# Attention scores on one core: which engine waits for the last stores at the end of the kernel

## The chip, the cores and the metric

The kernel runs on one core of a Trainium2 chip. The metric is the device time of one execution in microseconds. A core has five engines that each run their own list of instructions: TensorE (PE, with its weight loads listed apart as PEld), VectorE (DVE), ScalarE (ACT), GpSimd (POOL) and SyncE (SP). They meet only through semaphores: counters that an instruction or a DMA raises, and for which another instruction can wait.

## The reference

For each of 8 batches and 8 heads, the scores of 512 queries against 512 keys of 64 numbers, scaled by 1/8, all in float32:

```python
q = randn(8, 8, 512, 64); k = randn(8, 8, 512, 64)          # float32
scale = 1.0 / np.sqrt(q.shape[-1])
return np.einsum('bhqd,bhkd->bhqk', q, k) * scale           # (8, 8, 512, 512) float32
```

The inputs are 16.78 MB together, the output is 67.11 MB.

## The kernel before

The kernel uses no scheduler for its main part: each engine's list is written out by hand, one engine after the other in the source, with named semaphores between them (the function opens at the top of the file; all lines below are lines of the kernel before).

The batches are taken in 4 units of two batches. For each unit, SP loads 2 MB of k and 2 MB of q (L78, eight loads in all; the last two from L92). POOL casts each load to bf16 and regroups it (L122). PE turns the cast data by transposes against an identity (L130), DVE and ACT move the turned pieces out of PSUM into the operands kT and qz (L184). From these, PE makes the scores: 16 groups, each of 8 pairs of 128x512 products (L145). ACT takes the even pairs out of PSUM and DVE the odd ones, with the scale applied on the way (L209 and L212), into one of three store buffers named big. When both have finished a group, SP issues one store of 4 MB for it (L95 waits, L96 issues). So there are 16 stores, and store g raises the semaphore `store_sems[g % 3]` by 16 when it has landed.

The order on the engines' queues around the change is this:

- SP's list is: the loads, then 16 times a wait for ACT and DVE and a store, then the loop of L98 and L99, which waits for the final count of each of the three store semaphores (96, 80 and 80). In the program built from it these three waits are two instructions: one for the second store semaphore, one for the third and the first together. Nothing stands behind them on SP.
- PE's list is: a wait for the identity (L149), the first transposes, then the 16 groups of products with the transposes of later chunks between them. The last thing in it is the last product of group 15. PE already waits for earlier stores inside the groups (in `scores`, before the second product of a group), since a store buffer can be filled again only when its store has landed.
- ACT, DVE and POOL end with their last evacuation or cast, and none of them waits for the last stores.

What comes after an engine's last instruction of the kernel is not in the source: it belongs to the runtime, and shows in the trace only by the semaphores that it changes.

Of the kernel before, what the change touches and what calls it, by code (L numbers as in the profile page):

```python
# [5 lines left out]
def kernel(  # L6
# [5 lines left out]
    nc = tc.nc  # L12
# [27 lines left out]
    store_sems = [nc.alloc_semaphore(f"store{n}") for n in range(3)]  # L40
    ALL = CHUNKS * UNITS
# [24 lines left out]
    pe = nc.tensor  # L66
# [26 lines left out]
    for g in range(ALL):  # L93
# [1 line left out]
        nc.sync.wait_ge(sem["dve"], 4 * g + 4)  # L95
        nc.sync.dma_start(out=out_r[g], in_=store_buffer(g).rearrange("p x i k -> p x (i k)")  # L96
                          ).then_inc(store_sems[g % 3], 16)
    for n in range(3):  # L98
        nc.sync.wait_ge(store_sems[n], 16 * len(range(n, ALL, 3)))  # L99


    nc.gpsimd.memset(identity, 0.0).then_inc(sem["ident"], 1)  # L102
    nc.gpsimd.wait_ge(sem["ident"], 1)
# [24 lines left out]
    def turn(c, dst):  # L128
        for w in range(W):
            ins = pe.transpose(out=dst[:, w], identity=identity, in_=xw[:, c % SLOTS * W + w])  # L130
        ins.then_inc(sem["turn"], 1)

    def scores(g, p):
        x, i = p // 4, p % 4 * 2
        n = g % (2 * TILES) * 2 + x
        pair = PAIRS * g + p
        if pair >= 3:
            pe.wait_ge(sem["act" if p % 2 else "dve"], (pair - 3) // 2 + 1)
        for w in range(2):
            if p == 0 and w == 1:  # L140
                if g < 3:
                    pe.wait_ge(sem["ready"], (2, 6, 8)[g])
                else:
                    pe.wait_ge(store_sems[g % 3], g // 3 * 16)
            ins = pe.matmul(out=pss[pair % 3][:, w, :], lhsT=qz[:, n, i + w], rhs=keys[:, n],  # L145
                            start=True, stop=True)
        ins.then_inc(sem["pe_dve" if p % 2 else "pe_act"], 1)
# [7 lines left out]
    for g in range(ALL):  # L155
        c = g + CHUNKS
        for p in range(3):
            scores(g, p)
        if c < ALL:
            pe.wait_ge(sem["ready"], c // 2 + 1)  # L160
            turn(c, tp)
        for p in range(3, PAIRS):
            scores(g, p)
        if c < ALL:
            pe.wait_ge(sem["moved"], 4 * c + 4)

# [76 lines left out]
```

## Time and profile before

| what | before |
|---|---|
| median of 4 runs | 201.37 us (201.27 to 201.44) |
| the profiled execution's own time | 201.34 us |
| its span, from the first to the last instruction of the kernel | 200.0 us |
| mean granted clock of TensorE | 0.827 |
| busy: PE / DVE / ACT / POOL | 48% / 53% / 42% / 20% of the span |
| DMA moved | 83.95 MB, mean 420 GB/s |

The profile is one execution. Its page gives the busy time of each engine, the span cut in 40 slices with the busy share of engines and DMA in tenths, the DMA queues, the chain of work that ended last, and the costliest groups of instructions. Waiting instructions of a sequencer don't count as busy; they are listed when one asks for a source line or for the waits of SP's queue. Beside instructions, the trace records every change of a semaphore with its time, also those of the runtime before and after the kernel's own instructions.

### The profile page before, as it was taken

The page shows a single profiled execution, that of the slowest core. Times are in us where ns is not written, and L with a number is a line of the kernel's source. Part 1 is how long each engine was busy: PE and PEld are TensorE (multiplying, and loading weights), DVE is VectorE, ACT ScalarE, POOL GpSimd, SP SyncE. Part 2 cuts the span into 40 slices and gives each one's busy share as a digit, 9 for nine tenths or more (in the row PEclk, how much of TensorE's full clock was granted, in tenths as well). Part 3 has the DMA queues.
Part 4 walks back from the last instruction along what each step waited for, and adds up shares of the span by engine and source line. Part 5 has one row for each costly group of instructions (what it writes and reads, how often), then busy time and mean ns, then how long its engine had stood idle before and what let it go on. Part 6 is the DMA issues. An engine that isn't in the chain of part 4 may idle for free.

```text
span 200.0 us, 1081 instructions
## 1 busy us (share of the span) xinstructions
PE 96.4 (48%) x377; PEld 44.9 (22%) x384; DVE 106.0 (53%) x98; ACT 84.8 (42%) x97; POOL 39.5 (20%) x22
## 2 busy tenths in 40 slices
PE   0027550376785637576457636872737383810000
PEld 0026310142432214143124303330202020200000
DVE  0666790076797928476927682867363544440000
ACT  0205760264694726465626653664444443520000
POOL 0399999996000000000000000000000000000000
PEclk9999996588799978789958995799696969685555
DMA  6999999999999999999999999999999999999996
GB/s 193 426 436 429 439 419 432 429 410 426 432 442 426 419 434 437 432 419 429 436 436 426 419 442 442 423 419 439 439 429 419 432 432 429 429 419 439 423 432 269
DMA packets 5509, 83.95 MB, mean 420 GB/s; under 512 B 384, under 2 KB 384, under 8 KB 384
## 3 DMA queue, kind: packets, MB, share of 16 engines
q1 hardware_dynamic: 5504, 83.89, 98.6%
q8 instruction: 3, 0.05, 0.1%
q14 instruction: 2, 0.02, 0.0%
HBM read 16.78 MB, written 67.11 MB: 419 GB/s over the span
## 4 chain that ended last, share of the span: by engine, by line
DMA 54%; DVE 12%; POOL 12%; PE 10%; issue 1%; SPq 0%
DMA out_dram<-big 42%; POOL xb L122 12%; DVE big L212 10%; DMA big<-in_q_dram 7%; PE ps L145 7%; DMA big<-in_k_dram 4%; PE tp L130 2%; DVE qz L184 2%; DVE kT L184 1%; SPq L95 0%; SPq L87 0%; SPq L82 0%
## 5 line engine op out<-in xcount | busy, mean ns | idle before, releaser
L145 PE MATMUL ps<-kT,qz 128*128 128x512 bf16 x249 | 78.2, 445 | 64.8 <-DMA out_dram<-big 32.0
L212 DVE TENSOR_SCALAR big<-ps 128x1024 f32<-128x1024 f32 x64 | 76.9, 1222 | 53.2 <-PE ps L145 51.2
L209 ACT ACTIVATE big<-ps 128x1024 f32<-128x1024 f32 x64 | 65.0, 1024 | 72.2 <-PE ps L145 68.8
L145 PEld LDWEIGHTS ps<-kT,qz 128*128 128x128 bf16 x256 | 24.6, 108 | 111.4 <-DMA out_dram<-big 35.4
L122 POOL CAST xb<-big 128x2048 bf16<-128x2048 f32 x16 | 38.8, 2465 | 3.5 <-DMA big<-in_k_dram 3.0
L130 PE MATMUL tp<-identity,xb 128*128 128x128 f32 x104 | 18.8, 341 | 13.7 <-POOL xb L122 13.7
L130 PEld LDWEIGHTS tp<-identity,xb 128*128 128x128 f32 x104 | 17.1, 183 | 17.7 <-issue 16.5
L184 DVE COPY kT<-tp 64x512 f32<-64x512 f32 x14 | 9.7, 694 | 5.9 <-PE tp L130 5.4
L184 ACT COPY kT<-tp 64x512 f32<-64x512 f32 x14 | 8.1, 577 | 11.0 <-PE tp L130 10.7
L184 DVE COPY qz<-tp 64x512 f32<-64x512 f32 x12 | 8.3, 695 | 4.4 <-PE tp L130 4.0
L189 DVE MEMSET qz<- 128x4096 uint32 x2 | 6.9, 3472 | 6.8 <-PEq L87 6.0
L184 ACT COPY qz<-tp 64x512 f32<-64x512 f32 x12 | 7.4, 619 | 1.9 <-PE tp L130 1.8
L130 PE MATMUL ps<-identity,xb 128*128 128x128 f32 x24 | 3.9, 324 | 1.2 <-POOL xb L122 1.2
L130 PEld LDWEIGHTS ps<-identity,xb 128*128 128x128 f32 x24 | 3.5, 170 | 1.6 <-POOL xb L122 1.6
L184 ACT ACT_TABLE_LOAD x1 | 1.3, 1283 | 5.0 <-PEq L87 5.0
L184 DVE COPY qz<-ps 64x512 f32<-64x512 f32 x4 | 2.8, 695 | 0.9 <-PE ps L130 0.8
L184 ACT COPY qz<-ps 64x512 f32<-64x512 f32 x4 | 2.5, 624 | 1.1 <-PE ps L130 1.1
L184 DVE COPY kT<-ps 64x512 f32<-64x512 f32 x2 | 1.4, 694 | 0.3 <-PE ps L130 0.3
L184 ACT COPY kT<-ps 64x512 f32<-64x512 f32 x2 | 1.2, 578 | 0.6 <-PE ps L130 0.5
L102 POOL MEMSET identity<- 128x128 f32 x1 | 0.2, 204 | 4.6 <-POOLq L87 4.6
L104 POOL TENSOR_SCALAR_AFFINE_SELECT identity<-identity 128x128 f32<-128x128 f32 x1 | 0.3, 292 | 0.2 <-POOL identity L102 0.2
L229 POOL MEMSET const-float32-0.0<- 128x1 f32 x1 | 0.1, 98 | 0.2 <-issue 0.2
(3 smaller groups left out, 0.3 us busy)
## 6 DMA issues: line engine op xcount, KB each, us to landing
out_dram<-big SPq DMA_DIRECT2D x16, 4096.0 KB, 21.8
big<-in_k_dram SPq DMA_DIRECT2D x4, 2048.0 KB, 15.6
big<-in_q_dram SPq DMA_DIRECT2D x4, 2048.0 KB, 17.9
```

The source lines that it names most:

```text
L102: nc.gpsimd.memset(identity, 0.0).then_inc(sem["ident"], 1)
L104: nc.gpsimd.affine_select(out=identity, in_=identity, compare_op=mybir.AluOpType.not_equal, fill=1.0, base=0, pattern=[[-1, P]], channel_m ...
L122: cast = nc.gpsimd.tensor_copy(out=dst, in_=src)
L130: ins = pe.transpose(out=dst[:, w], identity=identity, in_=xw[:, c % SLOTS * W + w])
L145: ins = pe.matmul(out=pss[pair % 3][:, w, :], lhsT=qz[:, n, i + w], rhs=keys[:, n], start=True, stop=True)
L184: copy(out=dst, in_=src[:, h]).then_inc(sem["moved"], 1)
L189: engine.memset(qz[:, v * N:(v + 1) * N], 0.0).then_inc(sem["zeroed"], 1)
L209: lambda o, ps: nc.scalar.mul(out=o, in_=ps, mul=scale),
L212: lambda o, ps: nc.vector.tensor_scalar(out=o, in0=ps, scalar1=scale, scalar2=None, op0=mult),
L229: nc = _bacc.Bacc("TRN2", target_bir_lowering=False, num_devices=1)
```

## The change

The loop with the three final waits is taken from the end of SP's list and put at the end of PE's list. SP's list then ends with the issue of the last store. PE's list ends with two waiting instructions, the same pair as SP had: one for the second store semaphore, one for the third and the first. Nothing else is changed; the lists of ACT, DVE and POOL and all instructions ahead of the waits are the same.

```diff
@@ -95,9 +95,6 @@
         nc.sync.wait_ge(sem["dve"], 4 * g + 4)
         nc.sync.dma_start(out=out_r[g], in_=store_buffer(g).rearrange("p x i k -> p x (i k)")
                           ).then_inc(store_sems[g % 3], 16)
-    for n in range(3):
-        nc.sync.wait_ge(store_sems[n], 16 * len(range(n, ALL, 3)))
-
 
     nc.gpsimd.memset(identity, 0.0).then_inc(sem["ident"], 1)
     nc.gpsimd.wait_ge(sem["ident"], 1)
@@ -165,6 +162,10 @@
             pe.wait_ge(sem["moved"], 4 * c + 4)
 
 
+    for n in range(3):
+        pe.wait_ge(store_sems[n], 16 * len(range(n, ALL, 3)))
+
+
 
     def move(copy, c, s, tile_):
```

## The prediction

> **What bounds the kernel now.** I read the page's slices first, then the waits of SP's queue, then the waiting line itself, then the trace's record of semaphore changes behind the last instruction. The page, with the rows of PE, of its granted clock and of the DMA engines, and the main queue:
>
> ```profile
> span 200.0 us, 1081 instructions
> ...
> PE   0027550376785637576457636872737383810000
> ...
> PEclk9999996588799978789958995799696969685555
> DMA  6999999999999999999999999999999999999996
> ...
> q1 hardware_dynamic: 5504, 83.89, 98.6%
> q8 instruction: 3, 0.05, 0.1%
> ```
>
> The DMA row is full from the second slice to the last but one: the 84 MB set the time, and no engine does. PE's last four slices (5 us each) are empty. The end by stretches (us; busy time and count of PE, PEld, DVE, ACT, POOL; PE's clock; DMA share; GB/s):
>
> ```profile
> 178.00:198.00 20.00, 0.00 (x0) 0.00 (x0) 0.00 (x0) 0.00 (x0) 0.00 (x0) 0.51 1.00 427
> 198.00:200.00 2.00, 0.00 (x0) 0.00 (x0) 0.00 (x0) 0.00 (x0) 0.00 (x0) 0.50 0.12 49
> ```
>
> For the last 22 us nothing runs but the stores. The waits of SP's own queue (us in total, times, longest), and then the instructions of the line that the change takes away (shortest/median/longest in ns, start of the first and of the last in us):
>
> ```profile
> SPq L95 <- DVE big L212: 142.2, 16, 16.7
> ...
> SPq L99 <- DMA out_dram<-big: 22.1, 2, 19.4
> ```
>
> ```profile
> L99 SPq EVENT_SEMAPHORE  x2: 17/4852/9686, 180.6 to 190.3; - x2
> ```
>
> The first of the two waits passes at 180.6, the second is listed from 190.3 for 9.686 us, to 200.03, which is the end of the span. It has nothing to do but see the last store land.
>
> So the change can't touch the first 200 us. What it can move is the stretch behind the last landing: the profiled execution took 201.34 us, 1.34 more than its span. The record of semaphore changes shows what lies there. The last of the 16 steps of the first store semaphore comes at 200.006. Semaphore 2, which no line of the kernel uses, changes at these times (us from the span's start, listed by me from the trace):
>
> ```
> before the kernel      -0.371 -0.337 -0.299 -0.255 -0.231 -0.120 -0.081 -0.047  0.000
> first after it        176.174 176.742 176.780 177.629 200.149 200.193 200.231 200.265 200.312
> second after it       201.105 201.139 201.178 201.222 201.245 201.343 201.381 201.415 201.462
> ```
>
> Nine changes each time: a roll call of five engines, up in four steps and back in four. The first one after the kernel tells their order, since each engine answers when its list is empty and the one ahead has answered. 176.174 is 0.165 us after the step of PE's last product (176.009). 176.742 is 0.109 after ACT's last step (176.633). 176.780 follows 0.038 later and is POOL, idle for long. 177.629 is 0.145 after DVE's last (177.484). 200.149 is 0.143 after the last landing and is SP. So **the order is PE, ACT, POOL, DVE, SP, and back**. Between the two roll calls about 50 semaphores an engine are cleared; the last of the block 3 to 53, which starts latest and goes on longest, is cleared at 200.881, and PE, released last at 200.312, fits it.
>
> **The change part by part.**
>
> *Two waits leave SP.* Nothing is queued behind them, so SP is free for its answer at about 177.95 (last issue at 177.55, lasting 0.37, by the timeline). It gains nothing by that: its answer is the fifth, and waits for the four others. Cost 0; what covers it is the last store, 22 us.
>
> *Two waits come to PE.* Nothing of the kernel stands behind them, and PE's last product is done at 176.0. The first wait, passed at 180.6, lies beside 19.4 us of stores still under way: 0. The second passes when SP's did, at 200.006 plus PE's own lag. No instruction, DMA or queue moves otherwise, so all stores start and land as before: 0.
>
> *The answers behind the last landing.* Before, four of five had answered under the last stores; from the landing at 200.006 to the end of the first roll call at 200.312 it took 0.306 us (0.143 until SP answers, 0.163 for the four steps back). After, PE is late, it is the first in the row, and nobody behind it can answer. Three prices are needed.
>
> The lag of PE from landing to its answer does not stand in the trace as such. The waits that open the kernel show PE against the others (L87, same columns as above):
>
> ```profile
> L87 SPq EVENT_SEMAPHORE  x2: 17/17/17, 4.6 to 5.0; - x2
> L87 ACTq EVENT_SEMAPHORE  x2: 17/17/17, 4.6 to 5.0; - x2
> L87 DVEq EVENT_SEMAPHORE  x2: 21/21/21, 4.6 to 5.0; - x2
> L87 PEldq EVENT_SEMAPHORE  x2: 51/51/51, 4.6 to 5.0; - x2
> ```
>
> All four wait for one semaphore, raised at 4.537; the next instruction starts at 4.645 on SP and at 4.716 on PE, 0.071 later. After the roll call, SP starts to clear 0.135 after its release and PE 0.221: 0.086 later. From PE's last clear to its answer in the second roll call it is 0.224, after its last product 0.165. Bounds: 0.165 and 0.143 + 0.086 = 0.229. I take 0.143 + 0.071, about 0.215, since a wait that ends is the nearest row.
>
> The whole roll call from PE's answer to PE's release: 0.357 in the second (201.105 to 201.462), 0.371 before the kernel. A lower bound comes from adding the quickest step of each kind, 0.034 + 0.038 + 0.044 + 0.023 up and the 0.163 back of the first one: 0.302. I take 0.357, which is whole and without a wait in it.
>
> *Sum.* After: 0.215 + 0.357 = 0.572 from landing to release; before: 0.306. Difference **+0.27 us**, between 0.165 + 0.302 - 0.306 = +0.16 and 0.229 + 0.371 - 0.306 = +0.29. PE is released last and clears last in both kernels, so all behind it moves by the same. On the profiled execution that is 201.34 + 0.27 = 201.61; it lies 0.03 below the median, so 201.37 + 0.27 = **201.64 us**, 0.13% more. I count changes of up to 0.2% (0.40 us) as no change, about what a measurement of this kernel can tell.
>
> [...]
>
> **The rivals.**
>
> *A, the measured time ends before the roll call.* Then only PE's longer wait counts: its instruction lasts 51 ns against 17, and starts 11 ns later: +0.05, 201.42 us. Against it: the measured 201.34 reaches 1.31 beyond the last wait, nearly as far as the last answer at 201.46. For it: nothing in the profile says where the clock of the metric stops.
>
> *B, PE's sequencer slows down with the granted clock (the slower side).* The clock is 0.50 from 178 on, and it was 9 or more tenths in the rows at 4 to 5 us from which I took the lag. If everything of PE's answer took twice as long, its lag would be 0.43 and the total +0.27 + 0.215 = +0.49, 201.86 us; it decides from a lag of about 0.35. Against it: PE's first clear (0.221 after release) and its lag of 0.224 both fall at the 0.50 clock and are no longer than that.
>
> *C, PE has to fetch instructions behind the wait.* The queue named instruction moved three packets of 16 KB, in 0.88 to 0.99 us each, at 52.0, 97.4 and 150.6 us, when PE had 201, 450 and 687 recorded instructions behind it. If the next fetch fell behind the wait and nothing were fetched ahead, it would add up to 0.99: 202.6 us. Against it: the distance is 237 to 249 instructions, PE ends at 780, the clears add some 50, and the next fetch is due only near 924; two more instructions don't reach it.
>
> *D, I have the row of engines the wrong way round.* If PE answered last and SP first, the change would hide up the way what it now exposes, at most -0.16, 201.2 us. Against it: an SP that was first would have held back all of the answers at 176 and 177 us.
>
> **How the numbers follow.** Forecast: 0.68, of which 0.06 ends over 0.40 with the spread of the runs (0.17 between lowest and highest before). A: 0.08, within 0.2%. B: 0.13 and C: 0.05, slower. D: 0.06, half of it within 0.2% and half faster, should more be hidden than I can see. Same: 0.62 + 0.08 + 0.03 = 0.73; slower: 0.06 + 0.13 + 0.05 = 0.24; faster: 0.03. The range goes from A less the spread below the median before (201.42 - 0.09 = 201.33) to B with some of the spread (201.86 + 0.09 = 201.95); it leaves out C and D, and a little of B and of the forecast.
>
> **What would show it.** The span should grow by about 0.05 only, to 200.1, with the last instruction PE's wait of about 9.7 us from 190.3 in place of SP's, and the DMA row as full as before. In the semaphore record, the first roll call should lie wholly behind the last landing: first answer 0.17 to 0.23 after it, the whole 0.36 long, in even steps; clears and second roll call as long as before. An answer at 176 or 177 us would break the order that I read; a first answer over 0.35 after the landing is B, and an instruction packet behind 180 us is C. If stores land at another pace, the forecast is wrong in a place that I have put at nothing.

## The result and the profile after

| what | before | after |
|---|---|---|
| median | 201.41 us (201.27 to 202.32, 51 runs) | 201.71 us (201.53 to 202.32, 31 runs) |
| ratio to before | | 1.0016 (95% interval 1.0011 to 1.0021) |
| the profiled execution's own time | 201.34 us | 201.62 us |
| its span | 200.0 us | 200.0 us |
| time minus span, mean over the runs | 1.31 us (31 runs) | 1.58 us (32 runs) |

The change makes the kernel 0.30 us slower by the medians, 0.15%. That is within the 0.2% that was counted as no change, though the interval reaches to 0.21%. The kernel before was measured further beside the change, which is why its median here is 201.41 and not 201.37. The last row is the one to look at. It takes each run's own time and subtracts that run's own span, so a run whose stores happened to take longer doesn't disturb it. For the kernel before it is taken from the 31 runs measured beside the first four experiments, since the spans of the 51 are not on record. Behind the span, the change costs 1.58 - 1.31 = 0.27 us.

The page after the change, with the rows that answer to those of before:

```profile
span 200.0 us, 1081 instructions
...
PE   0027672386664768554864466662747475840000
...
PEclk9999998569999797996699697999585858585555
DMA  6999999999999999999999999999999999999996
...
q1 hardware_dynamic: 5504, 83.89, 98.7%
q8 instruction: 3, 0.05, 0.1%
```

The DMA row is as full as before, and the same three packets of instructions are there. PE's row differs in places, but its last four slices are as empty as before. The line that now waits, on PE in place of SP (shortest/median/longest in ns, first and last start in us):

```profile
L166 PEldq EVENT_SEMAPHORE  x2: 51/4868/9686, 180.6 to 190.3; - x2
```

It is the same pair of instructions as SP had, with the same 9.686 us of waiting; only the short one shows the engine, 51 ns against SP's 17. The waits of SP's queue no longer have a line for the final wait:

```profile
SPq L95 <- DVE big L213: 143.1, 16, 14.2
SPq L78 <- POOL xb L119: 23.1, 2, 18.5
SPq L230 <- PEq L230: 0.7, 1, 0.7
SPq L87 <- PEq L87: 0.5, 2, 0.3
```

So the page and the span of the profiled execution say that nothing happened. What did happen lies behind them, in the record of semaphore 2, the runtime's roll call. Here it is counted from the last step of the first store semaphore (200.006 before, 199.990 after), in us:

```
             PE        ACT       POOL      DVE       SP     | DVE    POOL   ACT    PE (release)
before      -23.832   -23.264   -23.226   -22.377    0.143  | 0.187  0.225  0.259  0.306
after         0.224     0.258     0.296     0.341    0.364  | 0.461  0.501  0.535  0.581
```

Before, four answers were given more than 22 us ahead of the last landing, and only the fifth and the way back were left. After, the whole row stands behind the landing, because the engine that asks first is the one that waits. PE is released 0.581 us after the landing and not 0.306: 0.275 us later. From there both go on alike: to PE's last clear (of the semaphores 3 to 53) it is 0.569 us before and 0.563 after. One stretch behind that differs in this profile: from its last clear to its answer in the second roll call PE takes 0.254 us and not 0.224. In the second profile of the change it is 0.224 again.

### The profile page after: what moved, and what is told of

The parts are those of the page before. It is cut to its first block, busy times and chain, and to the rows that moved or that the text cites. A ratio compares the mean times of both kernels' runs of the same rounds, so it can differ in the third digit from the quotient of the medians.

```text
span 200.0 us, 1081 instructions
## 1 busy us (share of the span) xinstructions
PE 103.0 (51%) x377; PEld 48.4 (24%) x384; DVE 106.1 (53%) x98; ACT 84.9 (42%) x97; POOL 39.5 (20%) x22
## 4 chain that ended last, share of the span: by engine, by line
DMA 54%; POOL 12%; DVE 11%; PE 11%; issue 1%; SPq 0%
DMA out_dram<-big 43%; POOL xb L119 12%; PE ps L142 9%; DVE big L213 8%; DMA big<-in_q_dram 7%; DMA big<-in_k_dram 4%; DVE qz L185 2%; PE tp L127 2%; DVE kT L185 1%; SPq L95 0%; SPq L87 0%; SPq L82 0%
## 5 line engine op out<-in xcount | busy, mean ns | idle before, releaser
L142 PE MATMUL ps<-kT,qz 128*128 128x512 bf16 x249 | 82.7, 470 | 59.2 <-DMA out_dram<-big 31.0
L142 PEld LDWEIGHTS ps<-kT,qz 128*128 128x128 bf16 x256 | 26.2, 112 | 108.8 <-DMA out_dram<-big 34.2
L127 PE MATMUL tp<-identity,xb 128*128 128x128 f32 x104 | 19.3, 348 | 13.8 <-POOL xb L119 13.8
L127 PE MATMUL ps<-identity,xb 128*128 128x128 f32 x24 | 5.6, 421 | 1.1 <-POOL xb L119 1.1
L127 PEld LDWEIGHTS ps<-identity,xb 128*128 128x128 f32 x24 | 5.0, 226 | 1.5 <-POOL xb L119 1.5
```

## The experiments

All are given with the same measures from their profile: the lag from the landing to the waiting engine's answer, the time from the landing to PE's release, and from there to PE's last clear. "Behind the span" is the mean of time minus span over all runs of a kernel. The kernel before, measured beside them, had 1.31 to 1.33 in each set.

| run | who is late | lag | landing to release | release to last clear | behind the span | median (before beside it) |
|---|---|---|---|---|---|---|
| before | SP | 0.143 | 0.306 | 0.569 | 1.31 | 201.41 |
| after | PE | 0.224 | 0.581 | 0.563 | 1.58 | 201.71 (201.41) |
| e1_act | ACT | 0.141 | 0.465 | 0.567 | 1.48 | 201.61 (201.41) |
| e2_dve | DVE | 0.182 | 0.423 | 0.565 | 1.42 | 201.49 (201.41) |
| e3_pool | POOL | 0.556 | 0.840 | 0.566 | 1.84 | 201.91 (201.41) |
| e4_pe_and_sp | PE and SP | 0.254 | 0.611 | 0.563 | 1.59 | 201.66 (201.41) |
| e5_pe_early | SP | 0.143 | 0.306 | 0.564 | 1.31 | 201.49 (201.37) |
| e6_warm_pe_waits | PE | 0.224 | 0.581 | 0.563 | 1.60 | 202.26 (201.37) |
| e7_warm_sp_waits | SP | 0.143 | 0.306 | 0.568 | 1.35 | 201.92 (201.37) |
| e8_change_again | PE | 0.224 | 0.581 | 0.563 | 1.58 | 201.80 (201.37) |
| e9_warm_40 | SP | 0.143 | 0.306 | 0.569 | 1.30 | 201.60 (201.38) |
| e10_fetch_only | SP | 0.142 | 0.306 | 0.562 | 1.34 | 202.07 (201.38) |
| e11_pool_awake | POOL | see below | 1.314 | 0.572 | 1.83 | 202.45 (201.38) |
| e12_waits_80 | SP | 0.142 | 0.306 | 0.563 | 1.31 | 201.62 (201.51) |

The theory was that an engine's place in the roll call, and its own lag, set the price. The first rival was that SP has to be the last, so that any other engine costs the same.

**The wait on each of the other engines.** The three lines leave SP and stand at the end of another engine's list (shown for ACT; with nc.vector for DVE and nc.gpsimd for POOL):

```diff
-    for n in range(3):
-        nc.sync.wait_ge(store_sems[n], 16 * len(range(n, ALL, 3)))
+    for n in range(3):
+        nc.scalar.wait_ge(store_sems[n], 16 * len(range(n, ALL, 3)))
```

On ACT:

> ScalarE, not TensorE, waits for the last stores. Theory (place in the roll call): ScalarE is second of five. Its lag from landing to answer is about SP's, 0.143 us, plus 0.005 (in the waits that open the kernel its next instruction starts at 4.650, SP's at 4.645); the roll call from its answer on lasts 0.357 - 0.034 = 0.323. Landing to PE's release: 0.47 us, against 0.306 before and 0.581 after the change; total +0.16 against before, about 201.57. Rival (SP must be last, whichever other engine waits costs the same): 0.58 and +0.28, about 201.69.

On DVE:

> VectorE waits for the last stores. Theory: fourth of five; lag 0.143 + 0.031 (its next instruction at 4.676 against SP's 4.645) = 0.174, and the roll call from its answer on 0.357 - 0.034 - 0.038 - 0.044 = 0.241. Landing to PE's release 0.415 us; total +0.11, about 201.52. Rival (SP must be last): 0.58 and +0.28, about 201.69.

On POOL:

> GpSimd waits for the last stores. Theory: third of five; lag taken as ScalarE's, 0.148, and the roll call from its answer on 0.357 - 0.034 - 0.038 = 0.285. Landing to PE's release 0.43 us; total +0.13, about 201.54. Rival (SP must be last): 0.58 and +0.28, about 201.69.

The waiting line of the three kernels, ACT, DVE and POOL:

```profile
L214 ACTq EVENT_SEMAPHORE  x2: 17/4852/9686, 180.7 to 190.4; - x2
```

```profile
L214 DVEq EVENT_SEMAPHORE  x2: 21/4850/9678, 180.6 to 190.3; - x2
```

```profile
L123 POOLq EVENT_SEMAPHORE  x2: 17/4856/9695, 180.8 to 190.5; - x2
```

These are the same two waits again, and nothing in the lines tells the three kernels apart beyond some ns. The record of semaphore 2 does, again from the last landing:

```
             PE        ACT       POOL      DVE       SP     | DVE    POOL   ACT    PE (release)
e1_act      -23.744     0.141     0.180     0.224    0.247  | 0.345  0.384  0.418  0.465
e2_dve      -22.813   -22.245   -22.207     0.182    0.205  | 0.303  0.342  0.376  0.423
e3_pool     -23.818   -23.327     0.556     0.600    0.623  | 0.720  0.760  0.794  0.840
```

The number of answers that are already in before the landing is one, three and two: the engine that waits is second, fourth and third. That confirms the order, each engine by its own kernel. For ACT and DVE the times are those expected, 0.465 for 0.47 and 0.423 for 0.415; the rival's 0.58 falls.

POOL is a miss. From its answer on, the rest of the row took 0.284 us, as worked out (0.285). Its lag, though, was 0.556 and not 0.148, so that POOL costs 0.53 behind the span, more than PE, although PE stands ahead of it. The place in the row is thus only one part of the price. The other is what an engine needs between its last instruction and its answer, and for POOL I had taken ACT's without a row of POOL's own.

**Both PE and SP wait.** SP keeps its waits, PE gets the same at the end of its list:

```diff
+    for n in range(3):
+        pe.wait_ge(store_sems[n], 16 * len(range(n, ALL, 3)))
```

> Both TensorE and SyncE wait for the last stores. Theory: TensorE alone decides, SP's early answer was worth nothing: as after the change, landing to PE's release 0.58 us, about 201.71. Rival (it is SP's early end that costs, by what SP or the runtime then does under the last stores): as before, 0.31 us, about 201.41.

Landing to release was 0.611 us, and 1.59 behind the span. PE alone decides, and SP's early end is worth nothing and costs nothing. PE's lag was 0.254 here, 0.03 more than in the three other profiles in which PE is late. PE's wait ends 0.034 us after the landing here as in the profile after the change, so the 0.03 lies between the end of the wait and the answer. The same two values, 0.224 and 0.254, stand ahead of PE's answer in the second roll call of the profiles before and after (in e6 and e10 it is 0.315 and 0.314 there); what decides between them was not found.

**PE waits, but not for the last.** As before, with two waits more on PE (one instruction in the program):

```diff
+    for n in (1, 2):
+        pe.wait_ge(store_sems[n], 16 * len(range(n, ALL, 3)))
```

> As before the change, SP waits for all three store semaphores, and TensorE waits as well, but only for the two that are complete by 190.3 us, not for the last store. Theory: waits on TensorE that pass 10 us before the last landing cost nothing: landing to PE's release 0.306 us, first four answers of the roll call under the last store, about 201.41. Rival (TensorE's added instructions cost by themselves, by more to fetch or to decode): 0.4 to 0.58 us and up to +0.28.

The first four answers lie 9.3 to 9.4 us ahead of the landing, and then it goes as before: 0.306, and 1.31 behind the span. The median was 201.49 against 201.37; with 1.31 behind the span, that difference is in the span itself (200.22 on average against 200.09), of which more below. The price is not in the waits on PE, but in their passing last.

**PE kept at work ahead of the end.** The changed kernel and the kernel before, both with 100 transposes more:

```diff
+    for w in range(100):
+        pe.transpose(out=tp[:, w % W], identity=identity, in_=identity)
```

> The changed kernel with 100 extra transposes of the identity into the free tile tp on TensorE ahead of its final waits (their result is used by nobody), so that it works until some 10 to 20 us after its last product. Theory: TensorE's lag is its sequencer's and does not depend on what the array did: lag 0.22, landing to release 0.58, about 201.71. Rival (the lag and TensorE's clears come from the long rest at the 0.50 clock): lag down to 0.15 or less and the stretch from release to last clear (0.563 after the change) down by 0.1 or more, 201.5 or less. Also, TensorE now passes the instruction at which the next packet of 16 KB is due; if it is fetched, it should be fetched during the transposes and cost nothing.

> The kernel before with the same 100 extra transposes on TensorE after its last product (their result is used by nobody); SP waits. Theory: TensorE still answers first, some 10 to 20 us later but under the last store; landing to release 0.306, release to last clear 0.569, about 201.41. Rival (TensorE's clears are slow from the long rest): release to last clear down by 0.1 or more, 201.3 or less.

From the second kernel's page:

```profile
PE   0027550475795639755767636762738283999300
```

The line of its transposes (shortest/median/longest in ns, first and last start in us):

```profile
L167 PE MATMUL tp<-identity x100: 272/273/273, 176.0 to 186.8; 128*128 128x128 f32 x100
```

PE works for 11 us longer, up to 187.0 in this kernel. PE's lag is the same in the first of the two kernels, 0.224, and the stretch of its clears within 5 ns in both, 0.563 and 0.568. So a rest of some 13 us instead of some 24 makes no difference to them; a PE that has hardly rested was not tried. What I wanted to see as well, PE at full clock when the store lands, was not reached: the records have it at 0.50 again from 190.7 (e6) and 191.9 (e7) on. What remains against rival B is that the lag of 0.224, at 0.50, is close to the 0.215 that I had worked out from rows at nine tenths. But both kernels have a longer span, 200.66 and 200.60 us on average against 200.09, which no theory had expected. The page has the packets of instructions as follows:

```profile
q8 instruction: 4, 0.07, 0.1%
```

The fourth packet, of 16 KB, moved at 187.6 us for 0.89 us. It came when PE's 987 or 988 recorded instructions were behind it, not at 924. It looked like the cause: a store has landed with the last of its 16 steps, and these are not even. In the kernel before, the sixteen steps of the last store come at 198.3 to 198.8 for twelve of them, and at 199.25, 199.53, 199.66 and 200.01 for four.

**The change once more.**

> The change itself once more, on the chip of these runs and with a second profile. Theory: landing to TensorE's answer 0.22, landing to release 0.58 us, release to last clear 0.56, +0.28 to +0.30 against before. Rival (the 0.28 was one profile's chance): the stretches differ by more than 0.05 from the first profile's.

All stretches repeat, 0.224, 0.581, 0.563, and 1.58 behind the span. The total is a miss: the medians differ by 0.43 us (201.80 against 201.37, 0.21%) and not by 0.28 to 0.30. Of that, 0.27 lies behind the span and 0.15 in it, of which more below.

**What made the span longer.** Three kernels, each from the kernel before, with SP waiting: 40 transposes, then 210 and 80 instructions that only look at semaphores (shown for 210; two waits make one instruction in the program):

```diff
+    for w in range(40):
+        pe.transpose(out=tp[:, w % W], identity=identity, in_=identity)
```

```diff
+    for w in range(210):
+        pe.wait_ge(sem["ident"], 2)
+        pe.wait_ge(sem["zeroed"], 2)
```

> The kernel before with 40 extra transposes of the identity into tp after TensorE's last product (result used by nobody) instead of the 100 that made the span 0.5 us longer; SP waits. With 40, TensorE ends 80 instructions later, at about 860, short of the fourth 16 KB packet of instructions. Theory (that packet holds up some of the 16 DMA engines, and the last store lands when the last of them is done): no fourth packet, the last landing as before, near 200.0, span 200.1, 201.4 us. Rival (the transposes themselves slow the stores): the span grows by 40% of 0.5 us, 200.3, 201.6 us.

> The kernel before with 210 instructions at the end of TensorE's list that only wait for semaphores whose counts were reached long ago (ident and zeroed); SP waits. No array work is added. Theory (the fourth packet of instructions holds up DMA engines): a fourth packet of 16 KB behind 176 us, the last landing at 200.5, span 200.6, 201.9 us. Rival (transposes slow the stores): span 200.1, 201.4 us.

> The kernel before with 80 instructions at the end of TensorE's list that only wait for counts reached long ago; SP waits. No array work, and TensorE ends short of the fourth packet of instructions. Theory (the span grows with the number of instructions that run beside the last stores, whatever they do: 80 transposed instructions gave +0.2 us, 200 to 210 gave +0.5 to +0.6): span 200.3, 201.6 us. Rival (two causes, the array work of the 40 transposes there and the packet in the run with 210 waits): span 200.1, 201.4 us.

The 40 transposes gave a mean span of 200.31 +- 0.02 against 200.09 +- 0.02 (standard errors of the means), with three packets: my theory of the packet fell. The 210 waits gave 200.72 with four packets, and with no array work at all: the rival fell too. The 80 waits, with three packets and no array work, gave 200.33 +- 0.03 against 200.19 +- 0.03 beside them. So some 80 instructions of either kind make the span 0.1 to 0.2 us longer, and 200 or 210 make it 0.5 to 0.6 us longer.

The traces also show when the stores fall behind. These are the times from one landing to the next for the last four stores, in us, beside the time at which PE's added instructions are done:

```
                  added work done    13th to 14th   14th to 15th   15th to 16th store
before            -                  9.836          9.703          9.680
e9_warm_40        180.8              9.925          9.731          9.680
e12_waits_80      184.0              9.842          9.807          9.680
e7_warm_sp_waits  187.0              9.996          10.004         9.689
e6_warm_pe_waits  187.2              9.995          9.977          9.689
e10_fetch_only    198.6              9.920          9.911          9.887
```

In the nine profiles without such work on PE, the last two columns lie at 9.67 to 9.72. They are longer by 0.1 us or more only where the added instructions run; e9's 9.731, behind its transposes, is 0.01 over. In e10 the fourth packet moved at 198.85 us, when the last store but one had already landed at 190.72 and not at 190.33, 0.40 of the 0.61 us by which the last landing is late. So neither the packet nor the array work is needed for the delay, and an estimate from the rows is 2 to 3 ns for each instruction (0.14 us for 80, 0.51 for 200, 0.63 for 210). Whether a packet adds a little stays open, and so does the way in which an instruction that only waits delays a store. One rival was not tried: all these runs are recorded ones, so a cost of recording the added instructions can't be told from a cost of the instructions.

**POOL at work ahead of its answer.** As the run with POOL, with 40 memsets behind a wait for the second last store:

```diff
+    nc.gpsimd.wait_ge(store_sems[2], 80)
+    for w in range(40):
+        nc.gpsimd.memset(xb[:, w], 0.0)
```

> GpSimd waits for the last stores, as in the run where its lag from the landing to its answer was 0.556 us, but it first waits for the second last store (about 190.3 us) and then zeroes 40 slices of xb that nobody reads any more, so that it has worked until a few us before the last landing. Theory (the 0.556 belongs to what GpSimd does ahead of its answer, each time): lag 0.5 to 0.56, landing to release 0.8 to 0.84, 201.9 us. Rival (it comes from GpSimd's rest of 150 us): lag near ScalarE's 0.14 or VectorE's 0.18, landing to release 0.43 to 0.47, 201.55 us.

```profile
L124 POOL MEMSET xb<- x40: 311/311/311, 190.4 to 200.3; 128x256 bf16 x40
```

The memsets followed each other every 0.253 us and took longer than I had meant. The last one ended at 200.566, behind the landing at 200.053, so the total can't be compared. The lag can: POOL answered 0.516 us after its last memset, and 0.526 after the end of its wait when it had rested for 150 us. The rest is not the cause; about 0.52 us goes by each time between POOL's last instruction and its answer, and in every other kernel here it is hidden, since POOL is done long before.

## Why the prediction was right

*The first 200 us are untouched.* Held: the DMA row, the last landing of the profiled execution (199.990 against 200.006) and the wait of 9.686 us are those of before. Over many runs it is less sharp. The mean span after the change is 200.19 +- 0.04 in the first set and 200.24 +- 0.04 in the second. The four sets of the kernel before have 200.09, 200.09, 200.12 and 200.19. Within one set, the change has 0.15 us more than the kernel before beside it (200.24 against 200.09), the kernel in which PE waits only for the second last store has 0.13 more, and the kernel with both waits 0.03 less (200.09 against 200.12). By the ends of the waits, 0.01 of it is PE's own (0.034 us after the landing against SP's 0.023). The rest, up to 0.14 us, is not settled: it is hardly more than what the sets of one kernel differ by, but larger than the error in its own set. It is why the medians differ by 0.30, and by 0.43 in the second set, and not by 0.27. So the prediction's term of 0 for the stores is shown for the profiled executions and open by some 0.1 us over many runs.

*Two waits leave SP: 0.* Shown by the run in which both wait: with SP late or early, PE late gives 1.58 to 1.60.

*Two waits on PE that pass early: 0.* Shown behind the span by the run in which PE waits for the second last store only (0.306 us, 1.31); its span is part of the open point above.

*PE's lag, taken as 0.215 from a wait at the start, bounds 0.165 and 0.229.* Measured 0.224, in three profiles, and 0.254 in one, which is above my bound. SP's lag, corrected by the opening waits, held within 0.01 for PE, ACT and DVE. For POOL, where ACT's was taken without such a row, it was 0.4 us off; so the sum for PE rested on PE having a row of its own.

*The whole roll call, 0.357.* Measured 0.357, from 0.224 to 0.581.

*The sum, +0.27.* Measured 0.275 from landing to release, and 0.27 behind the span over 32 runs. Predicted time 201.64, measured 201.71; the 0.07 are the 0.04 by which the median of before moved when it was measured further, and the unsettled part of the span.

*Rival A,* the time ends before the roll call: refuted, the time behind the span grew by 0.27. So the roll call is inside the measured time.

*Rival B,* PE's sequencer at half clock: not seen. The lag was 0.224 at the 0.50 clock, not 0.43. It was not tried with another clock at the same place.

*Rival C,* a fetch behind the wait: refuted, three packets as before, the last at 151.4. My point for the next packet, 924 instructions, was off, which the runs with more instructions show; it made no difference.

*Rival D,* the row the wrong way round: refuted by the three kernels with ACT, DVE and POOL.

The Trainium skill ("Runtime: NRT & Kernel Launch", section "The ~15µs preamble/postamble breakdown") gives 44 ns a hop over eight hops, about 355 ns, for the barrier ahead of a kernel. The trace has 0.371 us for that one and 0.357 for the second one behind the kernel. An estimate from the page's figure for the four steps that become visible here is 0.18 us.

Measured, these steps are 0.140 from PE's answer to SP's, and 0.217 back where it was 0.163 before. DVE's step back makes that difference: it takes 0.097 to 0.098 in the rows in which DVE has just answered, and 0.044 in those in which its answer lies far back.

## What to carry to other kernels

The end of a kernel is not the end of its span: when a change moves who finishes last, look at what the runtime does behind it, in the semaphores' record. If one engine has to wait for the last stores, let it be the one that is called last, here SP; from the waits on the others, the time got 0.11 us (DVE), 0.16 (ACT), 0.27 (PE) and 0.53 (POOL) worse. And where a page and a span say that nothing has changed, take each run's time minus its span, beside runs of the kernel before from the same set, before you call a small difference noise.

## What the runs showed of the hardware that was not expected

- POOL's answer in the roll call came about 0.52 us after its last instruction (0.526 and 0.516). From the last landing that was 0.556, where SP, ACT, DVE and PE took 0.14 to 0.25.
- Some 80 instructions more on PE beside the last stores, even if they only look at semaphores, made the span 0.1 to 0.2 us longer, and some 200 made it 0.5 to 0.6 us longer. The landings fall behind while these instructions run (9.81 to 10.00 us from one to the next in place of 9.67 to 9.72), and not at the packet of instructions.
- The 16 steps of a store's landing are not even: twelve within 0.5 us and four up to 1.3 us behind them, in the last two stores of the kernel before. What holds the four up was not found.
